# Tile 1 and tile 5 change places between the gathered and the dense part; groups of four keys; four more row buffers

## The chip, the core and the metric

The kernel runs on one core of a Trainium2 chip. The metric is the device time of one execution in microseconds (us), the median of several runs. The profile is of one further execution; its engines are TensorE (PE, with its weight loads as PEld), VectorE (DVE), ScalarE (ACT), GpSimd (POOL) and SyncE (SP). SP issues the plain DMAs, POOL the indirect ones; both run on the core's 16 DMA engines.

## What is computed

One decoder layer on 1024 tokens of width 1024. A mixer (a gated linear recurrence beside a gated linear attention) gives a sum with the input, which is normalised to x1. Then come a gate with a per-layer embedding (`ple`) and PEER, a mixture of 16384 one-neuron experts, and a second normalisation:

```python
q = (xt @ w_q).reshape(T, PEER_HEADS, 2, PEER_HALF)
s = jnp.einsum("thpc,hpkc->thpk", q, sub_keys)
top_s, top_i = lax.top_k(s, PEER_TOPK)
cand_s = top_s[:, :, 0, :, None] + top_s[:, :, 1, None, :]      # 256 a head
best_s, best_pos = lax.top_k(cand_s, PEER_TOPK)                 # 16 a head, 8 heads
expert_idx, gate = ..., jax.nn.softmax(best_s, axis=-1)
u = jnp.take(u_tab, ib, axis=0)                                 # (tokens, 128, 1024)
hid = gelu(jnp.einsum("td,ted->te", xb, u))
vv = jnp.take(v_tab, ib, axis=0)
out = jnp.einsum("te,ted->td", gb * hid, vv)
x = layer_norm(DN_ALPHA * x + out + ple)
```

Each token has 128 chosen experts; a row of `u_tab` or `v_tab` is 1024 floats (4 KB).

## The kernel before

The 1024 tokens are 8 tiles of 128, worked on in two halves (tiles 0 to 3, then 4 to 7). For each half run `mixer` and `post`. `post` multiplies by `w_out` (`pmix`), normalises to x1, transposes it, makes queries (`ppq`) and scores (`psc`), and then the `ple` gate in four blocks (`pplg`, `pplp`). After the second half comes `dense`.

PEER is done in two ways, by tile. **Gathered** (`GT`): `gather_u` fetches, for each of the 128 choices, the rows of `u` for 128 tokens in one indirect DMA (`ug`, 128x1024 floats, 512 KB; line 836), and DVE multiplies them by x1 and sums (L838). `gather_v` fetches the 128 rows of `v` of one token in one indirect DMA (`vg`, L865); when four have come, PE sums them by their weights into `ffn` in eight 32-column matmuls (L872, sixteen records in the trace: a *group* of four rows). A gathered tile so needs 128 `ug` and 128 `vg`, in 32 groups. **Dense** (`DT`): the four dense tiles are one block of 512 tokens, for which all 16384 experts are computed. `dense_gates` makes a table of gates for it ahead (`pg`, 128 matmuls a tile with ACT's `oi` and DVE's `one` and `oj`), written to `g_d`. In `dense`, `hidden` computes one key's 128 experts (`ph`, 24 matmuls), applies gelu, multiplies by the gates (`w`, L1026) and splits the product into a high and a low part (`wdh`, `wdl`); `value` adds those into the output (`pv`, 24 matmuls a key for each half of the width, in two halves), eight keys into one PSUM sum, which DVE then adds to `acc` (L1046). Weights come through SP as 256 KB pieces (`ur`, `vr`) that ACT and DVE split into `uh`/`ul`, `vh`/`vl`. `ph` and `pv` have 3072 matmuls each.

`route` makes a token's list of choices. For `DIRECT` tiles of a half it works from the scores at once, inside `post`; for the others the scores go through memory and routing is one of three streams (`us`, `routes`, `vs`) that `weave` takes in turn. `pump` lets a number of steps of this weave in beside each piece of other work, with a rate for each phase. `us` takes the tiles in the order of `GT`, and can begin one only when its half is scored and it is routed; `vs` begins a tile when its `u` part is complete. A scheduler then fixes one order for each engine, and each engine works strictly in its order: an instruction that waits holds up those behind it.

All gathered rows, and the two rows of the last normalisation, turn through one pool of 7 row buffers (`gath`). The ring of `wdh`/`wdl` has `RING` = 10 keys: eight of a group and two ahead. `GATES` says how many of the 32 pieces of the gate tables are made after each of `post`'s mix blocks (4), score heads (8) and `ple` blocks (4): 2, 1 and 4. The x1 of dense tiles of the first half is kept in `xs_d` and loaded ahead of `dense`.

The names that the prediction follows: lines 836 and 838 (`ug`), 865 and 872 (`vg`, `ffn`), 976 to 979 (gate table), 1026 and 1046 (`w`, `acc`).

Of the kernel before, what the change touches and what calls it, by code (L numbers as in the profile page):

```python
# [8 lines left out]
F32 = mybir.dt.float32  # L9
# [9 lines left out]
P = 128  # L19
T = 1024  # L20
D = 1024
# [9 lines left out]
KEYS = 128  # L31
# [2 lines left out]
RMS_EPS = 1e-6  # L34
NEG = -3.0e38

GT = (0, 1, 6, 7)
DT = (4, 5, 2, 3)
ND = 2

DIRECT = (2, 2)


ROUTE = 100
# [4 lines left out]
LATER = (0, 500, 500, -10000)  # L49

ROWS = 7
RING = 10

LOW = 60

TG = 8

GATES = (2, 1, 4)

ORDER = "GGAGGGGAAAGGAGaaGGGGG"  # L60
LEVELS = (1, 2, 4, 8, 16, 32, 64)
# [3 lines left out]
def kernel(ctx: ExitStack, tc: tile.TileContext, a: dict, out: bass.AP, tap=None):  # L65
    nc = tc.nc
# [65 lines left out]
    def row_bcast(t, src):  # L132
        nc.sync.dma_start(t, bass.AP(tensor=src.tensor, offset=src.offset, ap=[[0, P], [1, D]]))
        return t
# [97 lines left out]
    def pump(t):  # L232
        if flow["it"] is None:
            return
        flow["credit"] += t * flow["rate"]
        while flow["credit"] > 0:
            x = advance()
            if x is None:
                flow["it"] = None
                return  # L240
            if x < 0:
                flow["credit"] = 0.0
                return
            flow["credit"] -= x


    def split(h, l, src):
# [3 lines left out]
    def mm3(o, wh, wl, xh, xl, first, last):  # L251
        nc.tensor.matmul(o, wh, xh, start=first, stop=False)  # L252
        nc.tensor.matmul(o, wh, xl, start=False, stop=False)  # L253
        nc.tensor.matmul(o, wl, xh, start=False, stop=last)  # L254
# [575 lines left out]
    def gather_u(ti, idx, idxT, gate, H):  # L830
        x1 = peer.tile([P, D], F32, name="x1g")
        nc.sync.dma_start(x1, x1_d[ti])
        hid = small.tile([P, NSEL], F32, name="hid")
        for s in range(NSEL):
            ug = gath.tile([P, D], F32, name="ug", tag="rows")
            nc.gpsimd.indirect_dma_start(out=ug, out_offset=None, in_=a["peer_u"],  # L836
                                         in_offset=bass.IndirectOffsetOnAxis(ap=idx[:, s:s + 1], axis=0))
            nc.vector.scalar_tensor_tensor(ug, ug, 1.0, x1, op0=ALU.mult, op1=ALU.mult, accum_out=hid[:, s:s + 1])  # L838
            yield 1.46
        if tap:  # L840
            tap(f"hid{ti}", hid)
        nc.scalar.activation(hid, hid, AF.Gelu)
        nc.vector.tensor_mul(hid, hid, gate)
        H.append(hid)

    def gather_v(ti, idx, idxT, gate, H):
        ffn = ps_f.tile([P, D], F32, name="ffn")
        nc.tensor.transpose(ffn[:, :P], H[0], ident)
        pw = small.tile([P, P], F32, name="pw")
        nc.scalar.activation(pw, ffn[:, :P], AF.Copy)  # L850
        N = 4
        for ph in range(32 // N):

            w32 = peer.tile([P, 4, N, 32], F32, name="w32", bufs=2)
            nc.vector.memset(w32, 0.0)
            for c in range(4):
                dst = w32[:, c].rearrange("p r e -> p (r e)")[:, ph * N:ph * N + (N - 1) * 33 + 1:33]
                nc.vector.tensor_copy(dst, pw[:, 32 * c + ph * N:32 * c + ph * N + N])
            for r in range(N):

                rows_v = []
                for c in range(4):
                    t = 32 * c + ph * N + r
                    vg = gath.tile([P, D], F32, name="vg", tag="rows")
                    nc.gpsimd.indirect_dma_start(out=vg, out_offset=None, in_=a["peer_v"],  # L865
                                                 in_offset=bass.IndirectOffsetOnAxis(ap=idxT[:, t:t + 1], axis=0))
                    rows_v.append(vg)
                    if c < 3:
                        yield 1.46
                with ExitStack() as side:  # L870
                    for n, (e, c) in enumerate((e, c) for e in range(2) for c in (3, 0, 1, 2)):
                        mm = nc.tensor.matmul(ffn[32 * c:32 * c + 32, e * 512:(e + 1) * 512], w32[:, c, r],  # L872
                                              rows_v[c][:, e * 512:(e + 1) * 512], start=ph == 0 and r == 0,
                                              stop=ph == 32 // N - 1 and r == N - 1, skip_group_check=True)
                        if n == 0:

                            side.enter_context(tc.issue_after(mm.ins))
                            side.enter_context(tc.high_priority())
                yield 1.46
        ln2 = norm2()  # L880
        bt = gath.tile([P, D], F32, name="bt", tag="rows")
        st = small.tile([P, 2, 6], F32, name="st2")
        nc.sync.dma_start(bt, base_d[ti])
        for e in range(2):
            es = slice(e * 512, (e + 1) * 512)
            nc.vector.scalar_tensor_tensor(bt[:, es], bt[:, es], 0.5, ffn[:, es], op0=ALU.mult, op1=ALU.add)
            nc.vector.bn_stats(st[:, e], bt[:, es])
        finish(ti, bt, st, ln2)
# [53 lines left out]

    def norm2():

        return [row_bcast(gath.tile([P, D], F32, name=n, tag="rows"), a[n]) for n in ("ln2_g", "ln2_b")]

    def finish(ti, bt, st, ln2):
        layer_norm(bt, st, *ln2, 2)
# [36 lines left out]
    def dense(X):  # L985
        with ExitStack() as dctx:
# [5 lines left out]
            vps = dctx.enter_context(tc.tile_pool(name="vps", bufs=4, space=PSUM))  # L992
            acc = [a_p.tile([P, D], F32, name=f"acc{c}") for c in range(TT)]
            st = [a_p.tile([P, 2, 6], F32, name=f"std{c}") for c in range(TT)]
            NG = KEYS // 8

            def split_d(d_p, src, name, shape):
                raw = d_p.tile(shape, F32, name=f"{name}r")
# [3 lines left out]
                split(h, l, raw)  # L1002
                return h, l

            def load_g(g):
                G = []
                for q in range(2):
                    t = g_p.tile([P, 16, 8, 16], F32, name="gt", tag="g")
                    nc.sync.dma_start(t, g_d[g, :, 16 * q:16 * q + 16])
                    G.append(t)  # L1010
                return G

            def hidden(g, i, G):

                o = hps.tile([P, HT], F32, name="ph", tag="h")
                for n in range(2):
                    uh, ul = split_d(d_p, a["uT"][8 * g + i, :, 4 * n:4 * n + 4], "u", [P, 4, P])
                    for k in range(4):
                        mm3(o, uh[:, k], ul[:, k], X[0][:, 4 * n + k], X[1][:, 4 * n + k], n + k == 0, n * k == 3)
                if not G:  # L1020
                    G += load_g(g)
                w = d_p.tile([P, HT], F32, name="w", bufs=2)
                nc.scalar.activation(w, o, AF.Gelu)
                for q in range(2):
                    wq = w[:, 256 * q:256 * q + 256].rearrange("p (b t) -> p b t", t=16)
                    nc.vector.tensor_mul(wq, wq, G[q][:, :, i])  # L1026
                wh = d_p.tile([P, HT], F32R, name="wdh", bufs=RING)
                wl = d_p.tile([P, HT], F32R, name="wdl", bufs=RING)
                split(wh, wl, w)
                pump(5.2)  # L1030
                return wh, wl

            def value(g, W, e):
                es = slice(e * 512, (e + 1) * 512)
                o = [vps.tile([P, 512], F32, name=f"pv{c}", tag="v") for c in range(TT)]

                turns = [(i,) for i in range(8)] if g + 1 < NG or e == 0 else [(0,), (1,), (2,), (3,), (4,), (5, 6, 7)]
                for n in turns:
                    S = [split_d(v_p, a["peer_v"][(8 * g + i) * P:(8 * g + i + 1) * P, es], "v", [P, 512]) for i in n]
                    for c in range(TT):  # L1040
                        ts = slice(c * P, (c + 1) * P)
                        for i, (vh, vl) in zip(n, S):
                            mm3(o[c], W[i][0][:, ts], W[i][1][:, ts], vh, vl, i == 0, i == 7)
                    pump(2.6 * len(n))
                for c in range(TT):
                    nc.vector.scalar_tensor_tensor(acc[c][:, es], acc[c][:, es], 0.5 if g == 0 else 1.0, o[c],  # L1046
                                                   op0=ALU.mult, op1=ALU.add)
                    if g + 1 == NG:
                        nc.vector.bn_stats(st[c][:, e], acc[c][:, es])

            G = []
            W = [hidden(0, i, G) for i in range(8)]
            for c in range(TT):
                nc.sync.dma_start(acc[c], base_d[DT[c]])
            for g in range(NG):
                value(g, W, 0)
                Wn = []
                if g + 1 < NG:
                    G = load_g(g + 1)
                    Wn += [hidden(g + 1, i, G) for i in range(RING - 8)]  # L1060
                value(g, W, 1)
                if g + 1 < NG:
                    Wn += [hidden(g + 1, i, G) for i in range(RING - 8, 8)]
                W = Wn
            if flow["it"] is not None:
                drain(flow["it"])
# [105 lines left out]
```

## Time and profile before

| | us |
|---|---|
| median of three runs (3306.77 to 3309.68) | 3309.48 |
| profiled execution, own time | 3326.86 |
| its span, first to last instruction | 3325.1 |
| first half, then the second half's mixer (from 667) | 0 to 1130 |
| second half's `post`, with the gate tables | 1130 to 1574 |
| `dense`, first `ph` to the end of the last `pv` | 1574 to 3287 |
| from there to the end | 38 |

PE is busy 91% of the span, DVE 69%, ACT 37%, POOL 35%; the granted clock of PE is 0.951 on the mean. Busy times are read by stage: a wait matters only where it holds up the engine that sets that stage's length. A pipelined matmul's recorded duration (about 0.4 us) is longer than its pitch, so PE's work is counted by the distance between starts.

### The profile page before, as it was taken

The page shows a single profiled execution, that of the slowest core. Times are in us where ns is not written, and L with a number is a line of the kernel's source. Part 1 is how long each engine was busy: PE and PEld are TensorE (multiplying, and loading weights), DVE is VectorE, ACT ScalarE, POOL GpSimd, SP SyncE. Part 2 cuts the span into 40 slices and gives each one's busy share as a digit, 9 for nine tenths or more (in the row PEclk, how much of TensorE's full clock was granted, in tenths as well). Part 3 has the DMA queues.
Part 4 walks back from the last instruction along what each step waited for, and adds up shares of the span by engine and source line. Part 5 has one row for each costly group of instructions (what it writes and reads, how often), then busy time and mean ns, then how long its engine had stood idle before and what let it go on. Part 6 is the DMA issues. An engine that isn't in the chain of part 4 may idle for free.

```text
span 3325.1 us, 48007 instructions
## 1 busy us (share of the span) xinstructions
PE 3039.8 (91%) x17160; PEld 2321.9 (70%) x17160; DVE 2306.0 (69%) x5663; ACT 1232.4 (37%) x2130; POOL 1164.0 (35%) x1034
## 2 busy tenths in 40 slices
PE   8999988797999888758699999999999999999996
PEld 6788777676777675648477777777777767776663
DVE  7556558977788789989887866666666565664333
ACT  6443323263244464748533232232332222322221
POOL 0000000533421435551434544444444444543442
PEclk9999989898999898879899999999999999999998
DMA  5444444777877898977989999999999999998987
GB/s 173 146 165 152 138 165 132 289 280 269 308 249 245 297 306 303 336 266 222 346 318 326 333 337 333 342 341 345 332 333 344 333 330 341 325 331 313 315 290 253
DMA packets 364302, 939.73 MB, mean 283 GB/s; under 512 B 33920, under 2 KB 115968, under 8 KB 359968
## 3 DMA queue, kind: packets, MB, share of 16 engines
q0 software_dynamic: 147456, 536.94, 45.1%
q1 hardware_dynamic: 216608, 399.74, 34.6%
q8 instruction: 134, 2.20, 0.3%
q14 instruction: 104, 0.85, 0.1%
HBM read 854.76 MB, written 81.79 MB: 282 GB/s over the span
## 4 chain that ended last, share of the span: by engine, by line
PE 64%; DVE 14%; DMA 10%; issue 6%; ACT 4%; POOL 2%; another core or an unknown queue 0%; SPq 0%; POOLq 0%; DVEq 0%; ACTq 0%
PE ffn L872 6%; PE ph L253 6%; PE ph L254 6%; PE ph L252 6%; PE pv L253 6%; PE pv L252 6%; PE pv L254 6%; DMA vg<-in_peer_v_dram,idxT 3%; DVE ug L838 3%; DMA ug<-in_peer_u_dram,idx 3%; DMA vr<-in_peer_v_dram 1%; PE pg L977 1%; POOL ug L836 1%; POOL vg L865 1%; PE pgr L252 1%
## 5 line engine op out<-in xcount | busy, mean ns | idle before, releaser
L836 POOL DMA_INDIRECT ug<-in_peer_u_dram,idx x512 | 591.5, 1155 | 1338.5 <-DVE bs L765 614.6
L865 POOL DMA_INDIRECT vg<-in_peer_v_dram,idxT x512 | 571.2, 1116 | 791.7 <-DVE ug L838 360.7
L838 DVE SCALAR_TENSOR_TENSOR ug<-ug,x1g 128x1024 f32<-128x1024 f32 x512 | 622.1, 1222 | 279.0 <-DMA ug<-in_peer_u_dram,idx 213.5
L252 PE MATMUL ph<-x1hl,uh 128*128 128x512 f32 x1024 | 407.6, 398 | 2.4 <-ACT uh L248 2.1
L254 PE MATMUL ph<-x1hl,ul 128*128 128x512 f32 x1024 | 407.8, 398 | 0.0
L253 PE MATMUL ph<-x1hl,uh 128*128 128x512 f32 x1024 | 407.7, 398 | 0.0
L253 PE MATMUL pv<-vl,wdh 128*128 128x512 f32 x1024 | 404.0, 395 | 3.9 <-DVE vl L249 3.9
L254 PE MATMUL pv<-vh,wdl 128*128 128x512 f32 x1024 | 401.5, 393 | 0.0
L252 PE MATMUL pv<-vh,wdh 128*128 128x512 f32 x1024 | 376.6, 394 | 5.4 <-ACT wdh L248 2.9
L248 ACT ACTIVATE vh<-vr 128x512 fp32r<-128x512 f32 x256 | 160.9, 631 | 574.8 <-PE pv L254 304.0
L872 PE MATMUL ffn<-vg,w 128*32 128x512 f32 x2048 | 267.4, 643 | 73.7 <-DMA vg<-in_peer_v_dram,idxT 72.7
L249 DVE TENSOR_TENSOR vl<-vr,vh 128x512 fp32r<-128x512 f32 x256 | 174.9, 687 | 201.2 <-ACT vh L248 167.3
L248 ACT ACTIVATE uh<-ur 128x512 fp32r<-128x512 f32 x256 | 160.7, 629 | 335.5 <-PE ph L253 237.8
L249 DVE TENSOR_TENSOR ul<-ur,uh 128x512 fp32r<-128x512 f32 x256 | 175.2, 686 | 98.4 <-ACT uh L248 72.0
L253 PEld LDWEIGHTS pv<-vl,wdh 128*128 128x128 f32 x1024 | 193.0, 188 | 64.5 <-issue 13.0
L252 PEld LDWEIGHTS pv<-vh,wdh 128*128 128x128 f32 x1024 | 192.8, 189 | 61.8 <-issue 11.7
L253 PEld LDWEIGHTS ph<-x1hl,uh 128*128 128x128 f32 x1024 | 192.7, 188 | 61.3 <-issue 16.8
L254 PEld LDWEIGHTS ph<-x1hl,ul 128*128 128x128 f32 x1024 | 192.8, 188 | 60.2 <-issue 11.7
L252 PEld LDWEIGHTS ph<-x1hl,uh 128*128 128x128 f32 x1024 | 192.7, 188 | 58.4 <-issue 9.7
L254 PEld LDWEIGHTS pv<-vh,wdl 128*128 128x128 f32 x1024 | 193.1, 189 | 51.0 <-issue 10.7
L872 PEld LDWEIGHTS ffn<-vg,w 128*32 128x32 f32 x2048 | 55.8, 114 | 206.8 <-issue 123.2
L977 PE MATMUL pg<-oi,oj 128*128 128x128 f32 x1024 | 160.7, 297 | 39.2 <-ACT oi L976 21.9
(475 smaller groups left out, 6062.3 us busy)
## 6 DMA issues: line engine op xcount, KB each, us to landing
ur<-in_uT_dram SPq DMA_DIRECT2D x256, 256.0 KB
vr<-in_peer_v_dram SPq DMA_DIRECT2D x256, 256.0 KB
g_d<-gst SPq DMA_DIRECT2D x32, 1024.0 KB
gt<-g_d SPq DMA_DIRECT2D x32, 1024.0 KB
raw_zx<-in_w_z_dram SPq DMA_DIRECT2D x16, 512.0 KB
raw_zv<-in_w_v_dram SPq DMA_DIRECT2D x16, 512.0 KB
raw_zy<-in_w_z_dram SPq DMA_DIRECT2D x16, 512.0 KB
raw_ga<-in_w_z_dram SPq DMA_DIRECT2D x16, 512.0 KB
```

Of the source, the lines that this page charges most:

```text
L248: nc.scalar.activation(h, src, AF.Copy)
L249: nc.vector.tensor_tensor(l, src, h, op=ALU.subtract)
L252: nc.tensor.matmul(o, wh, xh, start=first, stop=False)
L253: nc.tensor.matmul(o, wh, xl, start=False, stop=False)
L254: nc.tensor.matmul(o, wl, xh, start=False, stop=last)
L836: nc.gpsimd.indirect_dma_start(out=ug, out_offset=None, in_=a["peer_u"], in_offset=bass.IndirectOffsetOnAxis(ap=idx[:, s:s + 1], axis=0))
L838: nc.vector.scalar_tensor_tensor(ug, ug, 1.0, x1, op0=ALU.mult, op1=ALU.mult, accum_out=hid[:, s:s + 1])
L865: nc.gpsimd.indirect_dma_start(out=vg, out_offset=None, in_=a["peer_v"], in_offset=bass.IndirectOffsetOnAxis(ap=idxT[:, t:t + 1], axis=0))
L872: mm = nc.tensor.matmul(ffn[32 * c:32 * c + 32, e * 512:(e + 1) * 512], w32[:, c, r], rows_v[c][:, e * 512:(e + 1) * 512], start=ph == 0 a ...
L977: nc.tensor.matmul(o[:, r], oj[:, t], oi, start=True, stop=True)
```

## The change

Tiles 0, 5, 6, 7 are gathered instead of 0, 1, 6, 7, and tiles 4, 1, 2, 3 dense instead of 4, 5, 2, 3. Three dense tiles are now of the first half, so `xs_d` holds three; `DIRECT` routes tiles 0, 1 and 4 in `post` and leaves 5, 6 and 7 to the weave; `GATES` puts 12 of the 32 gate pieces in the mix blocks (8 before), 8 in the scores and 12 in the `ple` blocks (16 before). In `dense` one PSUM sum takes 4 keys, so there are 32 groups of keys with 256 additions to `acc` (16 groups and 128 before), and the ring holds 6 keys. The gate table keeps its layout of 8 keys and is loaded after the first hidden block that needs it. A second pool, `more`, with 4 row buffers is opened in `dense`; of 11 rows that are asked for in turn 7 come from `gath` and 4 from `more`.

```diff
-GT = (0, 1, 6, 7)
-DT = (4, 5, 2, 3)
-ND = 2
-DIRECT = (2, 2)
+GT = (0, 5, 6, 7)
+DT = (4, 1, 2, 3)
+ND = 1
+DIRECT = (2, 1)
 ROWS = 7
-RING = 10
+MORE = 4
+KG = 4
+RING = 6
-GATES = (2, 1, 4)
+GATES = (3, 1, 3)
+    more = []
+    def row(name):
+        flow["rows"] = flow.get("rows", -1) + 1
+        pool = more[0] if more and flow["rows"] % (ROWS + MORE) >= ROWS else gath
+        return pool.tile([P, D], F32, name=name, tag="rows")
-            ug = gath.tile([P, D], F32, name="ug", tag="rows")
+            ug = row("ug")
-                    vg = gath.tile([P, D], F32, name="vg", tag="rows")
+                    vg = row("vg")
+            more.append(dctx.enter_context(tc.tile_pool(name="more", bufs=MORE)))
-            NG = KEYS // 8
+            NG = KEYS // KG
+            def load_g(g):
+                if g in G:
+                    return
+                G.clear()
+                G[g] = []
                 for q in range(2):
                     t = g_p.tile([P, 16, 8, 16], F32, name="gt", tag="g")
                     nc.sync.dma_start(t, g_d[g, :, 16 * q:16 * q + 16])
-                    G.append(t)
+                    G[g].append(t)
-                if not G:
-                    G += load_g(g)
+                load_g(i // 8)
-                turns = [(i,) for i in range(8)] if g + 1 < NG or e == 0 else [(0,), (1,), (2,), (3,), (4,), (5, 6, 7)]
+                turns = [(i,) for i in range(KG)] if g + 1 < NG or e == 0 else [(0,), (1, 2, 3)]
-                            mm3(o[c], W[i][0][:, ts], W[i][1][:, ts], vh, vl, i == 0, i == 7)
+                            mm3(o[c], W[i][0][:, ts], W[i][1][:, ts], vh, vl, i == 0, i == KG - 1)
-            W = [hidden(0, i, G) for i in range(8)]
+            W = [hidden(i) for i in range(KG)]
             for g in range(NG):
                 value(g, W, 0)
+                k = KG * (g + 1)
                 Wn = []
                 if g + 1 < NG:
-                    G = load_g(g + 1)
-                    Wn += [hidden(g + 1, i, G) for i in range(RING - 8)]
+                    load_g(k // 8)
+                    Wn += [hidden(k + i) for i in range(RING - KG)]
                 value(g, W, 1)
                 if g + 1 < NG:
-                    Wn += [hidden(g + 1, i, G) for i in range(RING - 8, 8)]
+                    Wn += [hidden(k + i) for i in range(RING - KG, KG)]
```

The order of POOL's queue from its first gather on, before (`ug` is a row fetch of the `u` part, `vg` of the `v` part, `idx` and `idxT` are the lists):

```order
masks.py:199 AFFINE_SELECT ident<-ident 128x128
L211 MEMSET qk_251 128x256
L836 DMA ug<-in_peer_u_dram,idx 128x1024 x129
L865 DMA vg<-in_peer_v_dram,idxT 128x1024
L836 DMA ug<-in_peer_u_dram,idx 128x1024
```

and the same place of the changed kernel:

```order
L214 MEMSET qk_251 128x256
L847 DMA ug<-in_peer_u_dram,idx 128x1024 x128
L876 DMA vg<-in_peer_v_dram,idxT 128x1024 x128
L847 DMA ug<-in_peer_u_dram,idx 128x1024 x114
L876 DMA vg<-in_peer_v_dram,idxT 128x1024
L847 DMA ug<-in_peer_u_dram,idx 128x1024 x15
L876 DMA vg<-in_peer_v_dram,idxT 128x1024
```

Before, the second gathered tile's `u` rows alternate with the first one's `v` rows. Now tile 0 is fetched whole, 128 and 128, and then 114 `u` rows of tile 5 stand in a block.

The end of PE's queue before (`pv` is a dense matmul of the last key group, `ffn` the matmuls of gathered rows of the last tile, 8 to a group of four rows):

```order
L252 MATMUL pv_28805<-vh,wdh 128x512
L253 MATMUL pv_28805<-vl,wdh 128x512
L254 MATMUL pv_28805<-vh,wdl 128x512
L252 MATMUL pv_28805<-vh,wdh 128x512
L872 MATMUL ffn<-vg,w_25485 32x512 x8
L253 MATMUL pv_28805<-vl,wdh 128x512
L254 MATMUL pv_28805<-vh,wdl 128x512
L252 MATMUL pv_28805<-vh,wdh 128x512
L253 MATMUL pv_28805<-vl,wdh 128x512
L254 MATMUL pv_28805<-vh,wdl 128x512
L872 MATMUL ffn<-vg,w_25485 32x512 x16
```

and in the changed kernel:

```order
L265 MATMUL pv_29154<-vh,wdl 128x512
L263 MATMUL pv_29154<-vh,wdh 128x512
L264 MATMUL pv_29154<-vl,wdh 128x512
L265 MATMUL pv_29154<-vh,wdl 128x512
L883 MATMUL ffn<-vg,w_24823 32x512 x32
L883 MATMUL ffn<-vg,w_25063 32x512 x32
L883 MATMUL ffn<-vg,w_25303 32x512 x32
L883 MATMUL ffn<-vg,w_25547 32x512 x32
L883 MATMUL ffn<-vg,w_25738 32x512 x32
L883 MATMUL ffn<-vg,w_25978 32x512 x32
```

Behind the last dense matmul stood 16 matmuls, two groups of four rows; now 192 stand there, 24 groups.

## Rows read from the trace of the kernel before

**Rows 1.** The page, 40 equal slices: tenths busy, and GB/s moved.

```profile
PE   8999988797999888758699999999999999999996
DMA  5444444777877898977989999999999999998987
```

**Rows 2.** Windows: stretch, PE, PEld, DVE, ACT, POOL busy (instructions), PEclk, DMA, GB/s.

```profile
1130.00:1253.00 123.00, 98.81 (x732) 85.21 (x728) 110.21 (x280) 81.14 (x182) 47.89 (x40) 0.91 0.91 312
1253.00:1360.00 107.00, 94.59 (x571) 69.97 (x571) 101.31 (x291) 60.47 (x129) 61.91 (x48) 0.91 0.92 321
1360.00:1574.00 214.00, 152.48 (x1079) 126.25 (x1078) 188.75 (x516) 138.39 (x333) 79.98 (x59) 0.85 0.82 266
1574.00:1743.00 169.00, 135.08 (x663) 100.60 (x662) 144.59 (x464) 76.76 (x156) 71.12 (x62) 0.88 0.94 328
1743.00:1869.00 126.00, 123.47 (x577) 91.58 (x576) 100.14 (x261) 39.70 (x65) 52.96 (x48) 1.00 0.91 326
1869.00:2107.00 238.00, 236.17 (x1114) 173.81 (x1113) 154.03 (x285) 70.13 (x119) 116.94 (x106) 1.00 0.94 338
2107.00:3138.00 1031.00, 1025.25 (x4879) 750.90 (x4879) 616.74 (x1127) 296.31 (x493) 472.56 (x438) 1.00 0.92 333
3138.00:3286.00 148.00, 147.60 (x762) 97.50 (x761) 51.78 (x97) 33.19 (x53) 66.11 (x67) 1.00 0.86 295
```

**Rows 3.** Windows of ug alone: DVE busy, POOL busy (issues), clock, DMA, GB/s.

```profile
0.00:1574.00 1574.00, 257.48 (x425) 267.06 (x214) 0.92 0.68 234
```

**Rows 4.** Windows of vg alone: PE, PEld, POOL busy (issues), clock, DMA, GB/s.

```profile
0.00:1574.00 1574.00, 54.46 (x336) 10.40 (x336) 111.28 (x86) 0.92 0.68 234
```

**Rows 5.** Timeline in dense: start, duration, engine, line, operation.

```profile
2097.96 0.40 PE L254 MATMUL ph<-x1hl,ul 128*128 128x512 f32 x1
2102.05 0.39 PE L253 MATMUL pv<-vl,wdh 128*128 128x512 f32 x1
2102.28 0.39 PE L254 MATMUL pv<-vh,wdl 128*128 128x512 f32 x1
2103.16 0.69 DVE L249 TENSOR_TENSOR wdl<-w,wdh 128x512 fp32r<-128x512 f32 x1 [0.76 <-ACT wdh L248]
2107.37 1.92 PE L872 MATMUL ffn<-vg,w 128*32 128x512 f32 x16
2109.23 0.50 PE L253 MATMUL pv<-vl,wdh 128*128 128x512 f32 x1
```

**Rows 6.** The page, DMA queues: packets, MB, time as share of 16 engines' span.

```profile
q0 software_dynamic: 147456, 536.94, 45.1%
```

**Rows 7.** Costliest groups: busy us, mean ns of one, idle before them and releasers.

```profile
L838 DVE SCALAR_TENSOR_TENSOR ug<-ug,x1g 128x1024 f32<-128x1024 f32 x512 | 622.1, 1222 | 279.0 <-DMA ug<-in_peer_u_dram,idx 213.5 <-issue 38.0 <-DMA x1g<-x_d 15.7
L249 DVE TENSOR_TENSOR ul<-ur,uh 128x512 fp32r<-128x512 f32 x256 | 175.2, 686 | 98.4 <-ACT uh L248 72.0 <-issue 15.3 <-PE ph L254 8.4
L1026 DVE TENSOR_TENSOR w<-w,gt 128x256 f32<-128x256 f32 x256 | 97.6, 422 | 10.8 <-issue 7.8 <-ACT w L1023 2.9
L1046 DVE SCALAR_TENSOR_TENSOR acc<-acc,pv 128x512 f32<-128x512 f32 x128 | 82.3, 680 | 22.4 <-issue 13.4 <-PE pv L254 9.0
L976 ACT ACTIVATE oi<-one,T 128x128 f32<-128x128 bf16 x512 | 165.5, 397 | 46.4 <-PE pg L977 20.4 <-DVE one L968 19.4 <-issue 4.8
L979 ACT ACTIVATE gst<-pg 128x512 f32<-128x512 f32 x128 | 133.8, 1060 | 18.6 <-PE pg L977 11.2 <-DMA g_d<-gst 3.7 <-PE pplg L253 2.2
```

**Rows 8.** Windows of pg alone: PE, PEld, ACT busy, clock, DMA, GB/s.

```profile
1130.00:1574.00 444.00, 133.91 (x864) 118.51 (x864) 112.12 (x107) 0.88 0.87 292
```

**Rows 9.** Timeline at the end.

```profile
3286.72 0.40 PE L254 MATMUL pv<-vh,wdl 128*128 128x512 f32 x1
3302.29 3.64 PE L872 MATMUL ffn<-vg,w 128*32 128x512 f32 x16 [8.64 <-DMA vg<-in_peer_v_dram,idxT]
```

**Rows 10.** Windows of a stretch with the first gathered rows; columns as rows 2.

```profile
620.00:640.00 20.00, 11.38 (x54) 10.60 (x55) 20.00 (x45) 0.71 (x3) 15.53 (x12) 0.69 0.98 363
```

**Rows 11.** Waits in 2107 to 3138: us in total, times, longest.

```profile
POOL vg L865 <- DVE ug L838: 170.3, 69, 9.1
```

More of the change, by code (lines that the diff above doesn't have):

```diff
@@ L880, in gather_v @@
         ln2 = norm2()
-        bt = gath.tile([P, D], F32, name="bt", tag="rows")
+        bt = row("bt")
         st = small.tile([P, 2, 6], F32, name="st2")
@@ L943, in norm2 @@
     def norm2():
-        return [row_bcast(gath.tile([P, D], F32, name=n, tag="rows"), a[n]) for n in ("ln2_g", "ln2_b")]
+        return [row_bcast(row(n), a[n]) for n in ("ln2_g", "ln2_b")]
     def finish(ti, bt, st, ln2):
@@ L1003, in split_d @@
                 return h, l
+            G = {}
             def load_g(g):
-                G = []
+                if g in G:
+                    return
+                G.clear()
+                G[g] = []
                 for q in range(2):
@@ L1009, in load_g, with hidden @@
                     nc.sync.dma_start(t, g_d[g, :, 16 * q:16 * q + 16])
-                    G.append(t)
-                return G
-            def hidden(g, i, G):
+                    G[g].append(t)
+            def hidden(i):
                 o = hps.tile([P, HT], F32, name="ph", tag="h")
                 for n in range(2):
-                    uh, ul = split_d(d_p, a["uT"][8 * g + i, :, 4 * n:4 * n + 4], "u", [P, 4, P])
+                    uh, ul = split_d(d_p, a["uT"][i, :, 4 * n:4 * n + 4], "u", [P, 4, P])
                     for k in range(4):
                         mm3(o, uh[:, k], ul[:, k], X[0][:, 4 * n + k], X[1][:, 4 * n + k], n + k == 0, n * k == 3)
-                if not G:
-                    G += load_g(g)
+                load_g(i // 8)
                 w = d_p.tile([P, HT], F32, name="w", bufs=2)
@@ L1025, in hidden @@
                     wq = w[:, 256 * q:256 * q + 256].rearrange("p (b t) -> p b t", t=16)
-                    nc.vector.tensor_mul(wq, wq, G[q][:, :, i])
+                    nc.vector.tensor_mul(wq, wq, G[i // 8][q][:, :, i % 8])
                 wh = d_p.tile([P, HT], F32R, name="wdh", bufs=RING)
@@ L1035, in value @@
                 o = [vps.tile([P, 512], F32, name=f"pv{c}", tag="v") for c in range(TT)]
-                turns = [(i,) for i in range(8)] if g + 1 < NG or e == 0 else [(0,), (1,), (2,), (3,), (4,), (5, 6, 7)]
+                turns = [(i,) for i in range(KG)] if g + 1 < NG or e == 0 else [(0,), (1, 2, 3)]
                 for n in turns:
-                    S = [split_d(v_p, a["peer_v"][(8 * g + i) * P:(8 * g + i + 1) * P, es], "v", [P, 512]) for i in n]
+                    S = [split_d(v_p, a["peer_v"][(KG * g + i) * P:(KG * g + i + 1) * P, es], "v", [P, 512]) for i in n]
                     for c in range(TT):
@@ L1049, in value @@
                         nc.vector.bn_stats(st[c][:, e], acc[c][:, es])
-            G = []
-            W = [hidden(0, i, G) for i in range(8)]
+            W = [hidden(i) for i in range(KG)]
             for c in range(TT):
```

## The prediction

> **What bounds the kernel now.** I read the page's slices first: from the middle on PE stands at 9 tenths and the DMA engines stand at 9 as well [rows 1]. So two resources are near their ends together, and the windows by stage must say which sets the pace [rows 2]. In the long stretch 2107 to 3138 PE is busy 1025 of 1031 us at the full clock (2.4 GHz), the DMA engines have a share of 0.92 at 333 GB/s, and DVE has 617 us. Since a recorded matmul is longer than its pitch, I count PE by starts: 0.23 us from one dense matmul to the next, and a group of four gathered rows holds PE from 2107.28 (one pitch after the last dense start) to 2109.23, so 1.95 us [rows 5]. This stretch has 1920 `ph`, 1964 `pv` and 62 groups: 3884 x 0.23 + 62 x 1.95 = 1014 us, 98% of it. PE bounds the dense stage, with DMA just under its own limit.
>
> `post` of the second half is different: DVE is busy 110 of 123, 101 of 107 and 189 of 214 us, PE only 99, 95 and 152 [rows 2]. There DVE's routing and row products hold PE up.
>
> How the rows come is the other thing to see. All 1024 gathers took 45.1% of 3325 us: 1.465 us each with the 16 engines to themselves, 0.524 MB each [rows 6]. Before the first `ph` 214 + 86 = 300 were issued [rows 3, 4]; 724 fell into `dense`. With the dense part's own 168 MB (512 pieces of 256 KB, 32 of 1 MB) that is 547 MB in 1712 us.
>
> **The change part by part**, against the profile's own time of 3326.9 us. The median of 3309.5 is 17 us lower; I carry the difference over unchanged. Counts of the changed kernel are from its order.
>
> *Gathers before dense.* Tile 5 can only start when the second half is scored, so tile 0's 256 gathers are all that can run ahead: 44 fewer than 300. In the mixer this takes off 15 row products but adds two groups: -3 us (between -10 and +4).
>
> *`post` of the second half.* Mix blocks: 64 more gate matmuls at 133.9 / 432 = 0.31 us (two records each) [rows 8], and five more groups: 20 + 10 us on PE, whose 99 become 129. ACT gets 64 x 0.40 + 16 x 1.06 = 43 us more [rows 7], 81 becomes 124. With PE at the 90% of the time that DVE now has there: 143 for 123, +20. Scores: DVE loses tile 5's selections and the products (about 34 of its 101 us), PE gets 23 gate matmuls and three groups, 13 us, to 108; I take 0. `ple` blocks: PE waits while two tiles are routed in a row; now one is. DVE goes down by 55 us, ACT keeps its work; half of PE's 62 idle us go: -30. In sum -10, with the mixer -13, between -45 (of PE's 98 idle us, 48 are filled by the added work and 45 go) and +25 (the mix blocks at DVE's pace on top of ACT's, and no gain behind).
>
> *First 40 keys of dense* (`ph` 1 to 960; before 169 + 126 + 238 = 533 us [rows 2]). The 78 gate matmuls that reached in here are done ahead, and no group stands in the first 20 keys. Keys 1 to 10: 240 `ph` and 172 `pv`, 95 us of PE, DVE about 128 with 45 products and tile 5's and 6's lists: 130. Keys 11 to 20: the block of `u` rows, 75 of them. DVE has 75 x 1.22 = 92 us of products, 10 x (5 x 0.69 + 2 x 0.42) = 43 of splits and gates, 20 x 0.68 = 14 of additions [rows 7], and some 25 of routing and the products' read-outs: 174. The DMA engines have 75 x 0.524 + 13 = 52 MB, at 333 GB/s 157 us. PE has 108. I take 170 for 126. Keys 21 to 40: DVE about 229 (routing of 6 and 7, 35 products, twice the additions), PE 236: 240 for 238. Sum 540, +7, between -40 and +45.
>
> *Keys 41 to 120* (1031 us before). Gathers and loads hold 340 MB in both orders, DVE gets 80 more additions (54 us; 617 becomes 671, beside PE). PE has 55 groups instead of 62: -14. The four more buffers can help where POOL waits for a product to free a row, 170 us in this stretch [rows 11], but rows need DMA time too. In a stretch with little else they came at 363 GB/s and a share of 0.98 [rows 10], so 340 MB need at least 937 us, and PE stays the longer: -15, between -31 (PE without a gap) and +64 (a rival below).
>
> The Trainium skill (Perfetto Trace Analysis, Optimization Strategy) says that equal gaps repeated along an engine that should be full can mean too few buffers; PE shows none here, POOL does. The Trainium skill (DMA: Bandwidth & Descriptors, Issuing engines are not separate DMA queues) has all queues interleave on the same 16 engines, which speaks against a gain from more rows in flight; by it this term is 0 and the sum 15 us higher.
>
> *Last 8 keys*, to the last `pv` (148 before). PE 432 x 0.23 + 12 x 1.95 = 123; DMA 58 rows and 14 MB, 44 MB, 132 us at 333: -16, between -25 and 0.
>
> *After the last `pv`.* This is the large term. Tile 7's `u` part ends later, its `v` rows begin with 96 `ph` to go (403 before), and 24 groups, 96 rows, stand behind PE's last dense matmul, where two stood. PE cannot take them earlier, and POOL can be ahead by 11 buffers at most. So 85 rows have yet to come: 85 x 1.465 = 125 us. After the last group's start came 23 us [rows 9]; `acc`'s normalisation can now lie beside the rows, so I add 25 with the group's wait. 150 instead of 38: +112, between +94 (85 rows at 363 GB/s, 1.44 us each, and 10) and +150 (96 rows at 1.67, as 12 were issued in those 20 us [rows 10], and 28).
>
> `xs_d` and its load grow by 1 MB each, 3 us of DMA at 333 GB/s, beside other work; I add nothing. The gate table's load is now queued on SP behind a key's `ur`, with 10 us of `pv` ahead of its first use.
>
> Sum: -13 + 7 - 15 - 16 + 112 = **+75 us**, 3402 in the profile's terms, **3385 us** as a median. The check by PE alone: 1413 us of dense matmuls and 72 groups, 140, are 1553 us up to the last `pv`, of 1688 forecast; before, 1413 + 105 x 1.95 + 24 = 1642 of 1712. PE loses cover because rows and routing come too late in the stage.
>
> **The rivals.** *Rows keep up* (faster). The 11 buffers and the lighter `post` let `dense` run at PE's 98% from its first `ph`: 1553 / 0.98 = 1585 to the last `pv`, -127; the end costs +106 at 363 GB/s; with -13 ahead, -34: **3275**. For it: POOL's waits for buffers, and DMA at 363 GB/s. Against: 526 MB in 1585 us is 332 GB/s on the mean, while the first 40 keys carry only 152 MB and DVE has 530 us of work in them. It decides if those keys take under about 470 us. The rule on gaps, above, points to this case.
>
> *The groups of four starve PE* (slower still). From a key's last `ph` (ends 2098.36) to its `wdl` (2103.85) take 5.5 us [rows 5]. In the new order only 36 dense matmuls, 8.3 us, stand between them and the first `pv` that reads it for about every fourth key; before, 104 and more. With twice the additions on DVE this can fail by 2 us in each of the 32 groups, and 64 us are lost: **3450**.
>
> *Nothing is left of it*: `post` gains its whole 45, the first 40 keys their 40, and the end is at its cheapest: **3310**.
>
> **How the numbers follow.** Forecast 0.70 (its own range 3345 to 3425), starved groups 0.15, rows keep up 0.10, nothing left 0.05. Faster by over 0.2% (what a measurement can tell apart): 0.10; within: 0.05; slower: 0.85. The range 3325 to 3450 holds the forecast's and the starved case's lower half.
>
> **What would show it.** In the profile after: some 125 us behind the last `pv` with GpSimd rows alone, PE waiting on `vg` there; at most 256 gathers ahead of the first `ph`; DVE over 90% busy in keys 11 to 20; `post` shorter by about 10 us. I am wrong if the tail is under 80 us, if `dense` up to the last `pv` is under 1620 us, or if PE waits on `wdl` by more than 30 us.

## The result and the profile after

The changed kernel takes 3331.45 us, the median of five runs (3327.49 to 3335.53), against 3309.48 (3301.99 to 3317.07) for the kernel before on the same chip: a ratio of 1.0063 with an interval of 1.0044 to 1.0082. It is slower by 22 us. The forecast was 3385 us, slower by 75: the sign was right, the size was not. The time also lies under the forecast's own range of 3345 to 3425.

The profiled execution of before lay 17 us above its median, and its unchanged copy (run e4 below) had a profiled execution only 3 above its own. So profiles are compared by stage, with the copy beside before. Each stage runs between the same matmuls in each trace (us, worked out from the timelines; the first half differs by 2 us or less). The scores begin here with the first `psc`, 30 us behind the border of [rows 2], so the forecasts of mix blocks and scores are best read as one, +20:

| stage | before | e4, its copy | after | forecast of the step | measured, by before / by e4 |
|---|---|---|---|---|---|
| second half's mixer | 463.4 | 460.0 | 450.9 | -3 | -12 / -9 |
| mix blocks | 153.4 | 147.3 | 155.4 | +20 | +2 / +8 |
| scores | 76.7 | 76.5 | 86.6 | 0 | +10 / +10 |
| `ple` blocks, to the first `ph` | 214.4 | 218.1 | 165.4 | -30 | -49 / -53 |
| first 40 keys | 532.3 | 530.5 | 512.2 | +7 | -20 / -18 |
| keys 41 to 120 | 1031.3 | 1030.2 | 1014.6 | -15 | -17 / -16 |
| last 8 keys, to the last `pv` | 148.6 | 148.8 | 123.8 | -16 | -25 / -25 |
| from the last `pv` to the end | 38.4 | 37.9 | 152.5 | +112 | +114 / +115 |
| span | 3325.1 | 3315.8 | 3329.7 | +75 | +5 / +14 |

Four places miss: `post` (mix blocks, scores and `ple` blocks) by 27 us, the first 40 keys by 27, and mixer and last keys by 9 each. The large term holds.

The page's slices of after, PE and DMA engines, answering to [rows 1]:

```profile
PE   8999989797999899997878999999999999999964
DMA  5444344787876999987998749989998998989898
```

The last two slices of PE fall to 6 and 4 while DMA stays at 9 and 8. The windows by stage of after, with the columns of [rows 2] (mix blocks, scores, `ple` blocks, keys 1 to 10, 11 to 20, 21 to 40, 41 to 120, the last 8, the tail; then `post` as one):

```profile
1119.00:1275.00 156.00, 139.04 (x1039) 114.30 (x1037) 128.91 (x278) 121.33 (x281) 59.69 (x48) 0.97 0.93 318
1275.00:1361.00 86.00, 86.00 (x574) 62.96 (x573) 54.12 (x147) 67.97 (x150) 31.29 (x28) 1.00 0.94 301
1361.00:1526.00 165.00, 135.83 (x1077) 116.42 (x1077) 134.35 (x370) 132.69 (x314) 44.46 (x29) 0.93 0.88 280
1526.00:1642.00 116.00, 103.18 (x413) 80.17 (x414) 112.22 (x316) 38.81 (x63) 61.97 (x47) 0.95 0.90 339
1642.00:1794.00 152.00, 122.37 (x470) 93.08 (x469) 152.00 (x374) 34.21 (x59) 91.11 (x75) 0.91 0.94 343
1794.00:2039.00 245.00, 240.85 (x1070) 188.08 (x1070) 209.41 (x563) 79.05 (x132) 71.18 (x65) 0.99 0.70 257
2039.00:3053.00 1014.00, 1014.00 (x4728) 741.26 (x4727) 686.27 (x1238) 288.00 (x485) 473.65 (x440) 1.00 0.91 334
3053.00:3177.00 124.00, 124.00 (x626) 85.37 (x626) 66.20 (x129) 32.61 (x53) 55.11 (x55) 1.00 0.88 316
3177.00:3330.00 153.00, 73.67 (x387) 13.45 (x385) 22.07 (x52) 1.36 (x5) 82.83 (x89) 0.66 0.90 346
1119.00:1526.00 407.00, 360.87 (x2685) 293.69 (x2681) 317.38 (x795) 321.99 (x742) 135.44 (x105) 0.96 0.91 299
```

Read the granted clock with the busy times: in `post` it is 0.93 to 1.00 where it was 0.85 to 0.91 [rows 2], and PE is never idle in the scores. DVE is busy all of keys 11 to 20 (152.00 of 152), which is the step where the block of `u` rows stands.

The gathers issued before the first `ph`, as windows of `ug` (DVE, POOL) and of `vg` (PE, PEld, POOL) alone; [rows 3, 4] had 214 and 86:

```profile
0.00:1526.00 1526.00, 153.97 (x256) 162.03 (x128) 0.95 0.69 235
0.00:1526.00 1526.00, 66.95 (x512) 13.88 (x512) 158.79 (x128) 0.95 0.69 235
```

128 and 128: tile 0 and nothing else, 44 fewer. The end, timeline of after, answering to [rows 9]:

```profile
3177.13 0.39 PE L265 MATMUL pv<-vh,wdl 128*128 128x512 f32 x1
3177.98 1.92 PE L883 MATMUL ffn<-vg,w 128*32 128x512 f32 x16 [0.46 <-DMA vg<-in_peer_v_dram,idxT]
3185.22 3.64 PE L883 MATMUL ffn<-vg,w 128*32 128x512 f32 x16 [5.32 <-DMA vg<-in_peer_v_dram,idxT]
...
3307.03 3.27 PE L883 MATMUL ffn<-vg,w 128*32 128x512 f32 x16 [3.04 <-DMA vg<-in_peer_v_dram,idxT]
```

Waits of after in 3177 to 3330 (us in total, times, longest):

```profile
PE ffn L883 <- DMA vg<-in_peer_v_dram,idxT: 59.6, 24, 6.7
POOL vg L876 <- PE ffn L883: 16.3, 18, 3.2
```

PE waits for rows before each of the 24 groups, and POOL waits for buffers for 16 of 153 us: here the transfers set most of the pace, 0.90 of the DMA engines at 346 GB/s.

### The profile page after: what moved, and what is told of

Same layout as the page of the kernel before. It is cut to its first block, busy times and chain, and to the rows that moved or that the text cites. A ratio compares the mean times of both kernels' runs of the same rounds, so it can differ in the third digit from the quotient of the medians.

```text
span 3329.7 us, 48075 instructions
## 1 busy us (share of the span) xinstructions
PE 3055.5 (92%) x17160; PEld 2315.7 (70%) x17160; DVE 2377.9 (71%) x5791; ACT 1230.0 (37%) x2132; POOL 1158.0 (35%) x1034
## 4 chain that ended last, share of the span: by engine, by line
PE 68%; DVE 17%; DMA 6%; ACT 4%; issue 4%; POOL 1%; SPq 0%; POOLq 0%; DVEq 0%; ACTq 0%
PE ffn L883 7%; PE ph L265 6%; PE ph L264 6%; PE ph L263 6%; PE pv L263 6%; PE pv L265 6%; PE pv L264 6%; DVE ug L849 6%; DMA vg<-in_peer_v_dram,idxT 3%; PE pg L988 2%; DMA sc<-sc_d 1%; PE ppq L263 1%; PE ppq L264 1%; PE pgr L263 1%; PE ppq L265 1%
## 5 line engine op out<-in xcount | busy, mean ns | idle before, releaser
L876 POOL DMA_INDIRECT vg<-in_peer_v_dram,idxT x512 | 563.1, 1100 | 763.0 <-PE ffn L883 435.5
L883 PE MATMUL ffn<-vg,w 128*32 128x512 f32 x2048 | 291.7, 667 | 73.7 <-DMA vg<-in_peer_v_dram,idxT 73.7
L1062 DVE SCALAR_TENSOR_TENSOR acc<-acc,pv 128x512 f32<-128x512 f32 x256 | 163.9, 681 | 71.6 <-PE pv L265 71.2
```

## The experiments

Each ratio is to the kernel before on the same chip; edits are shown by the values that change. My theory was the forecast's: the tile swap costs its tail, groups and buffers bring little. Later runs look for where the rest of the 75 us went.

**e1_swap: the tile swap alone**, groups of eight and 7 buffers as before.

```diff
-GT = (0, 1, 6, 7)  DT = (4, 5, 2, 3)  ND = 2  DIRECT = (2, 2)  GATES = (2, 1, 4)
+GT = (0, 5, 6, 7)  DT = (4, 1, 2, 3)  ND = 1  DIRECT = (2, 1)  GATES = (3, 1, 3)
```

> Tile swap alone: new GT, DT, ND, DIRECT and GATES; groups of 8 keys, ring of 10 and 7 row buffers as before. In its order 33 groups (132 gathered rows) stand behind the last dense matmul. Theory 'rows behind the dense work': (132 - 7) rows at 1.465 us and 25 us of closing are 208 us for 38 before, +170; post -48, first 40 keys -10, keys 41 to 128 -50 with fewer groups in them: about +60, 3370 us. Rival 'the groups of four cost it': without them the swap is a gain, 3290 us or below.

Measured 3405.89 us, ratio 1.0292 (1.0268 to 1.0316). The swap costs 98 us, more than the whole change. 33 groups, 132 rows, stand behind the last `pv` and take 304.3 us, 2.3 us a row: far slower than the 1.465 us of [rows 6]. Up to the last `pv` its profile is 177 us ahead of that of e4, the copy of before, 101 of them in the first 40 keys (429 us for 530); the tail costs 266 more. The window of that tail, columns as above:

```profile
3101.00:3406.00 305.00, 119.06 (x532) 20.68 (x530) 33.84 (x84) 3.53 (x9) 120.86 (x128) 0.61 0.73 247
```

**e2_group: groups of four and the four buffers alone**, on the old tiles (with the code that these values need).

```diff
-RING = 10
+KG = 4   RING = 6   MORE = 4
```

> Groups of four keys, ring of 6 and four more row buffers alone; tiles, DIRECT and GATES as before. 3 groups stand behind the last dense matmul, and 300 gathers ahead of the first. Theory 'rows behind the dense work': nothing moves there; PE stays the bound in dense, 3300 us (-20 to +5). Rival 'the groups of four cost it': PE waits for wdl and for acc, +22 us or more, 3330 us or above.

Measured 3296.07 us, ratio 0.9965 (0.995 to 0.998): a gain of 12 us, and the fastest version here that computes everything; it beats both kernels. Keys 41 to 120 go from 1031 to 1021 us, the last 8 from 149 to 136. PE has no idle time in the former:

```profile
2103.00:3124.00 1021.00, 1021.00 (x4814) 742.22 (x4813) 661.41 (x1206) 292.11 (x490) 473.63 (x441) 1.00 0.92 334
```

**e3_nomore: the changed kernel with 7 buffers.**

```diff
-            more.append(dctx.enter_context(tc.tile_pool(name="more", bufs=MORE)))
```

> The changed kernel without the pool of four more row buffers (7 buffers in all). 30 groups stand behind the last dense matmul instead of 24. Theory 'rows behind the dense work': 24 rows more at 1.465 us, less 6 groups x 1.95 us that leave the dense stretch, plus 4 rows less ready: +25 to +35 on the changed kernel's 3331, so 3360 us. Rival 'the buffers only move where POOL waits': 3331 us within 0.2%.

Measured 3415.67 us, ratio 1.0321 (1.0298 to 1.0344): a miss, 84 us over the changed kernel where I expected 25 to 35 or none. Up to the last `pv` it is no slower (keys 41 to 120 take 1004 us for 1014 with 55 groups in both, the last 8 keys 114 for 124 with five groups fewer); the loss is in the tail, 266.6 us for 30 groups. POOL and PE there, two timelines of e3:

```profile
3254.22 0.94 POOL L876 DMA_INDIRECT vg<-in_peer_v_dram,idxT  x1 [0.30 <-issue]
3259.17 0.94 POOL L876 DMA_INDIRECT vg<-in_peer_v_dram,idxT  x1 [4.02 <-PE ffn L883]
3260.41 0.94 POOL L876 DMA_INDIRECT vg<-in_peer_v_dram,idxT  x1 [0.30 <-issue]
3261.65 0.94 POOL L876 DMA_INDIRECT vg<-in_peer_v_dram,idxT  x1 [0.30 <-issue]
3262.90 0.93 POOL L876 DMA_INDIRECT vg<-in_peer_v_dram,idxT  x1 [0.31 <-issue]
3267.51 0.94 POOL L876 DMA_INDIRECT vg<-in_peer_v_dram,idxT  x1 [3.68 <-PE ffn L883]
```

```profile
3255.59 3.33 PE L883 MATMUL ffn<-vg,w 128*32 128x512 f32 x16 [5.35 <-DMA vg<-in_peer_v_dram,idxT]
3263.62 3.64 PE L883 MATMUL ffn<-vg,w 128*32 128x512 f32 x16 [4.70 <-DMA vg<-in_peer_v_dram,idxT]
```

It is a closed circle. The group ends at 3258.92 and frees four buffers; POOL issues four rows from 3259.17 on; the next group needs the first of these (three lay in the other buffers), and starts at 3263.62, 4.5 us after its issue. One turn is 8.0 us for four rows, 2 us a row, and each side waits for the other. Of the tail's 29 steps from group to group 27 last 7.9 to 9.0 us. The waits of POOL in 3141 to 3407:

```profile
POOL vg L876 <- PE ffn L883: 100.2, 29, 4.4
```

The Trainium skill (Perfetto Trace Analysis, Optimization Strategy) says that equal gaps repeated along an engine that should be full can mean too few buffers; by that rule this tail lacks them, and the trace agrees: POOL waits 100 us in 29 waits, 16 us with four buffers more.

**e11_more2: two more buffers instead of four.**

```diff
-MORE = 4
+MORE = 2
```

> The changed kernel with 2 instead of 4 more row buffers (9 in all); 26 groups behind the last pv. Theory 'buffers set the pace of the tail': a row takes as long as a buffer's round trip, some 16.2 us, over the buffers (2.31 us at 7, so 1.80 at 9, and no less than the engines' 1.465 at 11): 104 rows x 1.80 and closing are about 205 us for 153, 3375 us. Rival 'the DMA engines set it': 165 us, 3340 us.

Measured 3357.87 us, ratio 1.0146 (1.0122 to 1.017). The tail is 183.3 us for 26 groups, 1.76 us a row: between the two expectations. Its window:

```profile
3176.00:3360.00 184.00, 89.62 (x421) 16.89 (x417) 22.05 (x53) 1.36 (x5) 93.43 (x100) 0.72 0.88 319
```

So a row costs 2.2 us with 7 buffers (266.6 / 120), 1.76 with 9 (183.3 / 104) and 1.59 with 11 (152.5 / 96), each with the end's work in it.

**e5_tailcut: tile 7 sums 32 of its 128 `v` rows**; the other 96 are neither fetched nor summed.

```diff
-        for ph in range(32 // N):
+        PH = 32 // N if ti != GT[-1] else 2
+        for ph in range(PH):
```

> The changed kernel without 96 of tile 7's 128 gathered v rows (left out: the rows of 3 in 4 of its tokens); its order is the same up to the last dense matmul. Theory 'rows behind the dense work': from the last pv to the end about 30 us instead of 153, so 3331 - 123 = 3208 us. Rival 'the end is set by something beside the rows' (normalisation and output of the dense tiles, the last loads): 3260 us or above.

Measured 3203.87 us, ratio 0.9628 (0.9598 to 0.9657). In the profiles the tail goes from 152.5 to 21.0 us, by 131 for 123 expected, and the last 8 keys stay (124.5 for 123.8). The span falls by only 121, since the stages ahead took 10 us more in this execution; it ran on another chip, where before takes 3325.73 us for 3309.48. The rows cost what the tail shows, and nothing takes their place:

```profile
3188.00:3209.00 21.00, 0.01 (x1) 0.00 (x0) 16.80 (x27) 1.36 (x5) 0.00 (x0) 0.58 0.31 125
```

**e6_before21, e7_direct22, e8_group21: how many tiles are routed in `post`.** Does the gain of the `ple` blocks come from `DIRECT` alone? e6 is before, e8 is e2 with one tile fewer routed there; e7 is the changed kernel with one more.

```diff
-DIRECT = (2, 2)      # e6 on before, e8 on e2; e7 on after the other way round
+DIRECT = (2, 1)
```

> The kernel before with one edit: DIRECT (2, 1), so tile 5 (still dense) is routed by the weave and not in a row with tile 4 ahead of the ple blocks. 128 groups all stand ahead of the last pv. Theory 'routing in a row holds PE up in post': from the first pplg to the first ph about 175 us for 214, 3275 us (-25 to -40). Rival 'post gained by the gate pieces that moved': that stretch stays at 205 to 215 and the time at 3308 us.

> The changed kernel with DIRECT (2, 2): tile 5 is routed in post in a row with tile 4, as before, and its u rows may start ahead of dense (260 gathers ahead of the first ph for 256; 26 groups behind the last pv for 24). Theory 'routing in a row holds PE up in post': post gets 30 to 45 us longer, the tail 6 us: 3365 us. Rival 'tile 5's late start sets the end, wherever its routing is': 3310 us or below, since its rows come earlier.

> Groups of four, ring of 6 and four more buffers on the old tiles, with DIRECT (2, 1). No group stands behind the last pv. Theory: both gains add up, 3296 - 30 = 3266 us. Rival: a gain in post only brings the dense stage, which DMA and PE fill together, sooner to the same end: 3296 us.

e6: 3336.49 us, ratio 1.0022 (1.0005 to 1.0038), where a gain of 25 to 40 us was expected: a miss by some 40 us. e8: 3323.33, 0.9993 (0.9976 to 1.0009), 9 us behind the ratio of e2 where 30 were to be won: a miss too. In e6 the `ple` blocks gain 19 us, but not by less waiting: PE idles 59 us there for 62, and 366 gate records (`pg`) are made for 468. Tile 5 is a dense tile there, and its gate pieces need its routing. The first 40 keys lose 65 us, since routing and gate pieces come back there (256 records behind the first `ph` for 156):

```profile
1360.00:1555.00 195.00, 136.35 (x993) 110.66 (x991) 166.34 (x501) 111.35 (x261) 89.61 (x68) 0.85 0.92 306
1555.00:2152.00 597.00, 532.27 (x2525) 392.10 (x2526) 444.48 (x1117) 213.15 (x406) 271.29 (x239) 0.93 0.91 323
```

e7: 3356.73, 1.0088 (1.0063 to 1.0112), whose interval meets that of after. The `ple` stretch takes 205 us instead of 165; 34 of the 40 lie behind the last block, where PE stands longer before the first `ph` (57 us for 23). The windows of e7, up to the end of the last block and from there to the first `ph`:

```profile
1370.00:1518.00 148.00, 127.96 (x952) 117.13 (x951) 131.75 (x363) 127.73 (x308) 11.25 (x12) 0.94 0.60 180
1518.00:1575.00 57.00, 10.88 (x58) 5.83 (x59) 25.52 (x96) 3.21 (x7) 20.64 (x19) 0.62 1.03 398
```

The first 40 keys win 30 of the 40 back and the tail loses 14. So in the changed kernel the routing holds PE up as the theory has it, 66 us of idle time in the `ple` stretch for 29, but moved out of `post` it is moved, not removed. Over `post` and the first 40 keys together before takes 977 us (e4 972), after 920 and e7 934: 43 of the 57 us gained (38 of 53 by e4) are there without the routing's move and need another cause. e6 and e8 are no test of this, since there the routing of a dense tile moves.

**e10_gates214: the changed kernel with the old places of the gate pieces.**

```diff
-GATES = (3, 1, 3)
+GATES = (2, 1, 4)
```

> The changed kernel with GATES (2, 1, 4) as before: 8, 8 and 16 gate pieces in the mix blocks, the scores and the ple blocks for 12, 8, 12. 25 groups behind the last pv for 24. Theory 'row products and routing': post as a whole keeps its 407 us (mix blocks -15, ple blocks +15), 3331 us within 0.3%. Rival 'the gate pieces' places made the gain': post gets 25 us longer or more, 3356 us.

Measured 3336.86 us, ratio 1.0081 (1.0059 to 1.0104), with `post` 398 us for 407, 54 gate records fewer in it, and the first 40 keys 17 us longer: no gain of `post` lies in the pieces' places.

**e9_quietpost: before with few gathers in `post`.** The rate of the weave is 0 there; 25 `ug` and 25 `vg` still fall in, for 73 and 73.

```diff
-RATE = (0.8, 0.6, 1.0, 1.2)
+RATE = (0.8, 0.6, 0.0, 1.2)
```

> The kernel before with RATE[2] = 0: no gathered rows and no weave beside the second half's post (203 gathers ahead of the first ph for 300; 28 groups behind the last pv). Theory 'row products on DVE slow post, and PE's clock with it': from the first pmix to the first ph about 390 us for 444, with a granted clock of 0.95 or more for 0.88, though PE's matmuls are the same but for 11 groups. Rival 'post gained from the gate pieces and the routing that moved': it stays at 430 us or more. At the end, with 7 buffers, 112 rows at 2.3 us as in the runs with 7 buffers: 250 us for 38, so 3440 us in all; rival '1.465 us a row': 3350 us.

Measured 3430.02 us, ratio 1.0367 (1.0344 to 1.039), with 28 groups in a tail of 246.7 us for the 250 expected. `post` falls from 444 to 372 us, where I expected about 390, at a clock of 0.93 instead of 0.95 or more. The windows of its `post` and tail:

```profile
1127.00:1499.00 372.00, 309.53 (x2184) 269.60 (x2182) 340.17 (x950) 276.86 (x638) 69.64 (x51) 0.93 0.67 213
3180.00:3427.00 247.00, 98.46 (x450) 16.98 (x448) 21.40 (x52) 1.36 (x5) 98.33 (x105) 0.63 0.73 248
```

**e13_thinpost: before with thin products in `post`.** The rows are fetched as before, but DVE multiplies only 8 of their 1024 columns while `post` runs; the other columns' products are left out.

```diff
+            C = slice(0, 8 if flow["phase"] == 2 else D)
-            nc.vector.scalar_tensor_tensor(ug, ug, 1.0, x1, ..., accum_out=hid[:, s:s + 1])
+            nc.vector.scalar_tensor_tensor(ug[:, C], ug[:, C], 1.0, x1[:, C], ..., accum_out=hid[:, s:s + 1])
```

> The kernel before, with the row product of the 71 u rows that fall beside the second half's post taken over 8 of the 1024 columns (left out: the other columns of these products). The gathers stay: 305 ahead of the first ph for 299, and 8 groups stand behind the last pv for 2. Theory 'the products' time on DVE slows post': 71 x 1.1 us less on DVE, and from the first pmix to the first ph 390 to 405 us for 444, with a granted clock of 0.92 or more for 0.88. Rival 'the rows' transfers slow post' (they went too in the run without rows beside post): 430 us or more, at 0.88. The end gets longer by some 30 rows at 2.2 us: 3308 - 45 + 50 = about 3315 us in all.

Measured 3296.33 us, ratio 0.9908 (0.9873 to 0.9944), 25 us under before. `post` takes 426 us, between the two expectations, but it holds more: 2537 matmul records instead of 2381, since all gate pieces that used to reach into `dense` are made. With the first 40 keys it is 921 us instead of 977. Its window, and that of before over all of `post`:

```profile
1130.00:1556.00 426.00, 357.71 (x2537) 299.72 (x2535) 357.50 (x1159) 319.37 (x741) 168.58 (x148) 0.94 0.95 319
```

```profile
1130.00:1574.00 444.00, 345.88 (x2381) 281.44 (x2377) 400.27 (x1085) 280.00 (x643) 189.79 (x146) 0.88 0.87 292
```

The DMA share rises to 0.95, PE idles 68 us instead of 98, and the stage is still shorter: the rows' transfers were not what held it up, DVE's products were.

**e12_kg2: groups of two keys, 13 buffers, on the old tiles** (the last group's turns follow). Does the gain of e2 grow?

```diff
-KG = 4   RING = 6   MORE = 4
+KG = 2   RING = 4   MORE = 6
```

> A version that may beat both: old tiles with groups of 2 keys, ring of 4 and 6 more row buffers (13). All 128 groups stand ahead of the last pv. Theory 'PE fills dense there, buffers only smooth it': 3296 us (group of four) minus 0 to 15. Rival 'short groups starve PE': 64 changes of sums and a chain of wdl with 4 keys' room cost 30 us or more, 3325 us.

Measured 3350.45 us, ratio 1.0126 (1.0106 to 1.0147), 54 us over e2: slower, as the rival had it, and by more. Keys 41 to 120 take 1109 us; their window:

```profile
2125.00:3234.00 1109.00, 1090.42 (x5105) 752.95 (x5104) 750.65 (x1370) 285.26 (x499) 513.58 (x482) 0.99 0.91 333
```

17 groups more than in e2 fall in here (1250 records of `ffn` for 972), some 34 us, and PE is listed idle for 19. The other 35 of the 88 us are small losses, by starts 8 us in `ph`, 12 in `pv` and 12 in the groups, that the waits don't name; they stay open.

**e4_copy: before, unchanged.**

> The kernel before once more, unchanged, for a second profile. If the 17 us by which its profiled execution lay over the median of its runs belong to that execution, this profile's own time is 3300 to 3318; if profiling costs them, it is near 3327 again. The ratio is 1.000 within 0.2%.

Measured 3314.22 us, ratio 1.0008 (0.9991 to 1.0026). This is how far two equal kernels differ here.

## Why the prediction was right in sign and wrong in size

**Tail: right.** 24 groups and 96 rows stood there as counted, and 112 us forecast are 114 measured; e5 takes 131 us away with them. But the 1.465 us a row hold for 11 buffers only (1.59 with the end's work in it): in e1, with 7, the same sum gives (132 - 7) x 1.465 + 25 = 208 us for 304. The number of buffers was a hidden condition, and that the change brought enough of them was luck.

**`post`: mis-sized**, -10 forecast, -37 measured (-35 by e4). Of 444 us PE was busy 345.9 and idle 98. I let the added gate matmuls and groups put 48 us on top of the old busy time, 394, and left 40 idle. The idle time came out near the forecast (407 - 361 = 46 us). In the `ple` blocks it went from 62 to 29 us, the half that was forecast, and e7 puts that down to the routing. DVE's relief came too: no `ug` is multiplied in `post` any more, where 73 took 88.6 us, and DVE's 400 us are 317. The step that failed is the sum on PE: 360.9 us instead of 394, 15 us added instead of 48. With every record counted to the start of the next, the gate matmuls went from 112 to 124 us (868 records, then 1024), the groups from 48 to 54 (18, then 27), the transposes `pt` from 8 to 4, and all others stayed at 179. So the added work was too dear: I had taken 0.31 us a gate matmul from the recorded time of `pg`, but by starts it is 0.26 in before and 0.24 in after, and the added work costs 37 us. And the old work did not keep its price: it fell by 22 us, half of it in the groups, from 2.6 us each to 2.0. Windows of `ffn` alone in `post` (PE, PEld, DVE, ACT), before and after:

```profile
1130.00:1574.00 444.00, 48.71 (x292) 9.06 (x288) 0.00 (x0) 0.00 (x0) 0.88 0.87 292
1119.00:1526.00 407.00, 55.80 (x436) 11.53 (x432) 1.28 (x2) 0.00 (x0) 0.96 0.91 299
```

The granted clock rose from 0.88 to 0.96 on the mean, but not all of the busy time can be scaled by it: `pplg` alone takes 61.70 us in before and 61.61 in after, for the same 384 matmuls. PE waited 36.9 us for `vg` rows in before's `post`, 13.8 in after and 4.9 in e13, where a group costs 2.05 us too, as 36.90 us for 288 records. So relief from the products brings the cheaper groups without any swap. Whether the clock granted behind a wait is what makes a group dear, no run here separates. Mix blocks and scores, +20 forecast, came out at +12 (+18 by e4); the scores, taken at 0, had 4 us of idle PE for 14 us more work and grew by 10.

**First 40 keys: mis-sized**, +7 forecast, -20 measured. Keys 1 to 10, 11 to 20 and 21 to 40 took 116, 152 and 245 us for 130, 170 and 240 forecast. Keys 1 to 10 held 36 products and not 45. Keys 11 to 20 are bound by DVE as said, but I had summed DVE's recorded durations, and these overlap. Three starts in a row of DVE in after:

```profile
1661.51 0.68 DVE L260 TENSOR_TENSOR vl<-vr,vh 128x512 fp32r<-128x512 f32 x1
1662.12 0.68 DVE L260 TENSOR_TENSOR wdl<-w,wdh 128x512 fp32r<-128x512 f32 x1
1662.72 1.24 DVE L849 SCALAR_TENSOR_TENSOR ug<-ug,x1g 128x1024 f32<-128x1024 f32 x1
```

An operation recorded with 0.68 starts 0.61 or 0.60 before the next one. Over 2107 to 3138 of before the durations add up to 682 us, for 617 in which DVE was busy [rows 2]: 10% too much. In keys 11 to 20 of after they add up to 178 us, near my 174, for 152 in which DVE was busy. For PE I had counted by starts for this reason, and not for DVE.

**Keys 41 to 120: right** (-15, measured -17), by the count of groups; PE is busy all 1014 us. That the four buffers bring nothing here is shown by e3, which has 7 and takes 1004 with the same 55 groups. Since the -15 came from that count, the prediction's sentence that the term would be 0 if more rows in flight bring nothing did not follow. **Last 8 keys:** -25 instead of -16; PE's sum of 123 us was met (124), while I had let DMA's 132 set the stage.

**The mixer:** -12 (-9 by e4) for -3. It goes with the tiles: the second half's first `pmix` stands at 1114 to 1122 us in all runs with the new ones and at 1124 to 1130 in all with the old. What in them does it, no run here separates.

**The base.** "I carry the difference over unchanged" took 17 us of the miss out of sight: before's profiled execution lay 17 us above its median, after's at its own. From profile to profile the forecast is off by 70 us (+75, measured +5), from median to median by 53.

**The rivals.** Starved groups: PE waits on `wdl` for 7 us in all of after, so it falls for groups of four; in groups of two something of that size happens (e12), but the waits don't name `wdl`. Rows keep up: false, 1651 us of `dense` to the last `pv`. Nothing is left: the nearest in its mechanism, since `post` gained most of its bound of 45 and the first 40 keys half of theirs. But its 3310 us do not follow from its own bounds: with the mixer and `post` at -45, the first 40 keys at -40 and the tail at +94 the sum of +75 becomes -22, 3287 us. None of the three signs of being wrong came (tail 152 us, `dense` 1651, `wdl` 7): they guarded the mechanism and not the sizes.

What the change does, then: the swap takes 98 us (e1) by putting rows behind the last dense matmul, more than it wins ahead of it, and the four buffers, worth 12 us together with groups of four on the old tiles (e2), are worth 84 in the new arrangement (e3), since that tail runs at the pace of the buffers.

## What to carry to other kernels

Gathers that can't start before late results end up behind the work that should cover them: count which rows can be issued ahead, and price those left at the tail's own pace. That pace is set by the buffers first (issue, landing, use, free as one turn), and by the engines' time only when there are enough of them. A busy time that is carried over to a changed stage holds for work that does not stand beside waits; work that does can get cheaper when the waits go, as the groups did here. Count an engine's work by its starts and not by recorded durations.

## What the runs showed of the hardware

- Row pace by buffers: 2.2, 1.76 and 1.59 us for 512 KB with 7, 9 and 11 of them, at 248, 319 and 346 GB/s. The Trainium skill (DMA: Bandwidth & Descriptors, Issuing engines are not separate DMA queues) has all queues interleave on the same 16 engines; by that more rows in flight bring nothing where the engines are full, as in keys 41 to 120, but the tail's share was 0.74 with 7 buffers, and there they bring 84 us.
- PE's matmuls of a group take 3.64 us in the tail at a granted clock of 0.66 on the mean, between its two levels of 1.2 and 2.4 GHz, and 1.92 in `dense` at full clock.
- Relief for DVE showed on PE as less idle time and a higher granted clock (98 to 68 us and 0.88 to 0.94 in e13), and the groups in that stage became cheaper (2.7 to 2.05 us by their windows), while the matmuls of `pplg` did not in after (61.70 and 61.61 us).
